# Batch norm with ReLU on one core: one tile of 32 rows per partition, and all loads then all stores on one queue

## Chip, cores, metric

One core of one Trainium2 chip. The metric is the device time of one execution in microseconds (us), lower is better. The granted clock was 1.00, so it plays no part. "Share" and "GB/s" of DMA mean the 16 DMA engines of the core together. In the views, ACT is the scalar engine, PE the tensor engine (PEld its weight loads), DVE the vector engine, POOL GpSimd and SP the sync engine. A load moves data from HBM (the chip's main memory) to SBUF (the core's own memory, 128 partitions), a store moves it back. "The turn" is the place in one queue where the first stores stand directly behind the last loads.

## The reference

```python
def setup_inputs():
    batch, channels, h, w = 32, 128, 32, 32        # x: 16.8 MB of float32
    ...
def reference(x, gamma, beta, running_mean, running_var, eps):
    normalized = (x - running_mean[None, :, None, None]) / np.sqrt(running_var[None, :, None, None] + eps)
    scaled = normalized * gamma[None, :, None, None] + beta[None, :, None, None]
    return np.maximum(scaled, 0).astype(np.float32)
```

x is 4,096 rows (batch x channel) of 1,024 numbers. Each row needs one scale and one bias, so a row is one ACT instruction: relu(scale * x + bias), 128 rows at a time, one in each partition. 16.8 MB go in and 16.8 MB come out.

## The kernel before

Two tiles of 16 rows per partition, loaded in pieces on the sync queue. ACT works in place and issues the stores from its own queue, so loads and stores run side by side. Cuts are marked.

```python
J = 16
PIECES = (((0, 2), (2, 4), (4, 8), (8, 16)), ((0, 8), (8, 16)))
STORE_CUTS = {(0, 1)}
...
    xr = x.rearrange("b c h w -> (b c) (h w)").rearrange("(t p j) w -> t p j w", p=P, j=J)
...
    for t in range(T):
        for a, b in PIECES[t]:
            xt = data.tile([P, b - a, HW], F32, name=f"x{t}_{a}")
            nc.sync.dma_start(out=xt, in_=xr[t, :, a:b, :])
            tiles.append((t, a, b, xt))
...     # parameters: four small loads on the scalar queue, one matmul that spreads them, sqrt, reciprocal, ...
    with tc.manual_schedule(engines={mybir.EngineType.Activation}):
        for t, a, b, xt in tiles:
            first = a
            for j in range(a, b):
                nc.scalar.activation(out=xt[:, j - a, :], in_=xt[:, j - a, :], func=ACTF.Relu,
                                     bias=bias_t[:, j : j + 1], scale=scale_t[:, j : j + 1])
                if j + 1 == b or (t, j + 1) in STORE_CUTS:
                    nc.scalar.dma_start(out=outr[t, :, first : j + 1, :], in_=xt[:, first - a : j + 1 - a, :])
                    first = j + 1
```

Of the kernel before, what the change touches and what calls it, by code (L numbers as in the profile page):

```python
# [1 line left out]

# [4 lines left out]


F32 = mybir.dt.float32
ACTF = mybir.ActivationFunctionType  # L10



J = 16

PIECES = (((0, 2), (2, 4), (4, 8), (8, 16)), ((0, 8), (8, 16)))

STORE_CUTS = {(0, 1)}


@with_exitstack
def kernel(
    ctx: ExitStack,
    tc: tile.TileContext,
    x: bass.AP,
    gamma: bass.AP,
    beta: bass.AP,
    running_mean: bass.AP,
    running_var: bass.AP,
    eps: bass.AP,  # L30
    out: bass.AP,
):
    nc = tc.nc
    B, C, H, W = x.shape
    HW = H * W
    P = nc.NUM_PARTITIONS
    assert C % J == 0 and P % (C // J) == 0 and (B * C) % (P * J) == 0
    Q = C // J
    T = B * C // (P * J)

    xr = x.rearrange("b c h w -> (b c) (h w)").rearrange("(t p j) w -> t p j w", p=P, j=J)
    outr = out.rearrange("b c h w -> (b c) (h w)").rearrange("(t p j) w -> t p j w", p=P, j=J)

    data = ctx.enter_context(tc.tile_pool(name="data", bufs=1))
    params = ctx.enter_context(tc.tile_pool(name="params", bufs=1))
    psum = ctx.enter_context(tc.tile_pool(name="psum", bufs=1, space=bass.MemoryType.PSUM))

    tiles = []
    for t in range(T):
        for a, b in PIECES[t]:  # L50
            xt = data.tile([P, b - a, HW], F32, name=f"x{t}_{a}")
            nc.sync.dma_start(out=xt, in_=xr[t, :, a:b, :])  # L52
            tiles.append((t, a, b, xt))



    raw = params.tile([Q, 4, J], F32, name="raw")
    for k, src in enumerate((running_var, gamma, running_mean, beta)):
        nc.scalar.dma_start(out=raw[:, k, :], in_=src.rearrange("(q j) -> q j", j=J))
    eps_t = params.tile([P, 1], F32, name="eps_t")  # L60
    nc.vector.memset(eps_t, float(eps))  # L61
    rep = params.tile([Q, P // Q, Q], F32, name="rep")
    nc.gpsimd.memset(rep, 1.0)  # L63
    nc.gpsimd.affine_select(  # L64
        out=rep,
        in_=rep,
        compare_op=mybir.AluOpType.is_equal,
        fill=0.0,
        base=0,
        pattern=[[0, P // Q], [-1, Q]],  # L70
        channel_multiplier=1,
    )
    cols = psum.tile([P, 4, J], F32, name="cols")
    nc.tensor.matmul(  # L74
        cols.rearrange("p k j -> p (k j)"),
        rep.rearrange("q r s -> q (r s)"),
        raw.rearrange("q k j -> q (k j)"),
        start=True,
        stop=True,
    )  # L80
    std_t = params.tile([P, J], F32, name="std_t")
    nc.scalar.activation(out=std_t, in_=cols[:, 0, :], func=ACTF.Sqrt, bias=eps_t[:, 0:1], scale=1.0)  # L82
    rstd_t = params.tile([P, J], F32, name="rstd_t")
    nc.vector.reciprocal(out=rstd_t, in_=std_t)  # L84
    scale_t = params.tile([P, J], F32, name="scale_t")
    nc.vector.tensor_mul(out=scale_t, in0=cols[:, 1, :], in1=rstd_t)  # L86
    ms_t = params.tile([P, J], F32, name="ms_t")
    nc.vector.tensor_mul(out=ms_t, in0=cols[:, 2, :], in1=scale_t)  # L88
    bias_t = params.tile([P, J], F32, name="bias_t")
    nc.vector.tensor_sub(out=bias_t, in0=cols[:, 3, :], in1=ms_t)  # L90

    with tc.manual_schedule(engines={mybir.EngineType.Activation}):
        for t, a, b, xt in tiles:
            first = a
            for j in range(a, b):
                nc.scalar.activation(  # L96
                    out=xt[:, j - a, :],
                    in_=xt[:, j - a, :],
                    func=ACTF.Relu,
                    bias=bias_t[:, j : j + 1],  # L100
                    scale=scale_t[:, j : j + 1],
                )
                if j + 1 == b or (t, j + 1) in STORE_CUTS:
                    nc.scalar.dma_start(
                        out=outr[t, :, first : j + 1, :], in_=xt[:, first - a : j + 1 - a, :]
                    )
                    first = j + 1


# [1 line left out]
_INS = ['x', 'gamma', 'beta', 'running_mean', 'running_var', 'eps']  # L111
_OUTS = [((32, 128, 32, 32), 'float32')]

_NUMBERS = {'eps': 1e-05}


# [26 lines left out]
```

## Time and profile before

| | before |
|---|---|
| time, median (range) | 83.86 us (83.78 to 83.91, 3 runs) |
| span of the profiled run | 81.9 us |
| DMA share, both queues | 96.2% |
| ACT busy | 38.5 us (47%) |

Read it as a DMA kernel: 33.56 MB through engines that are busy nearly all the time. The lines are in the prediction.

The view counts each packet whole in the stretch in which it begins. Of this kernel's stretches of 5 us some therefore read 367 and some 500 GB/s, but their DMA share goes along (0.86 and 1.16).

### The profile page before, as it was taken

What the parts mean: (1) busy time and instruction counts of PE and PEld (TensorE: products, weight loads), DVE (VectorE), ACT (ScalarE), POOL (GpSimd) and SP (SyncE); (2) the same over time, 40 slices, a digit from 0 to 9 for tenths busy, and PEclk for the clock granted to TensorE, in tenths of its full rate; (3) what the DMA queues carried; (4) which work ended last, traced back from release to release, by engine and by line L of the source; (5) the groups of instructions that cost most, each with busy time, mean ns of one, the idle gap of its engine ahead of it and who ended that gap; (6) DMA issues with size and microseconds to landing.
All of it is one profiled execution on the core that took longest, in us unless ns stands there. A gap on an engine that the chain in (4) does not pass through costs nothing.

```text
span 81.9 us, 119 instructions
## 1 busy us (share of the span) xinstructions
PE 0.7 (1%) x2; PEld 0.5 (1%) x2; DVE 0.8 (1%) x5; ACT 38.5 (47%) x34; POOL 0.8 (1%) x6
## 2 busy tenths in 40 slices
PE   0002000000000000000000000000000000000000
PEld 0002000000000000000000000000000000000000
DVE  0000300000000000000000000000000000000000
ACT  0600377799039999199994199993000000000000
POOL 3000000000000000000000000000000000000000
DMA  2899999989899999979789798996999899799690
GB/s 32 328 425 472 408 448 448 512 352 494 370 448 416 446 418 396 500 296 600 320 380 580 304 464 384 512 512 288 480 512 400 368 512 448 320 512 496 272 512 0
DMA packets 1936, 33.56 MB, mean 410 GB/s; under 512 B 272, under 2 KB 272, under 8 KB 528
## 3 DMA queue, kind: packets, MB, share of 16 engines
q1 hardware_dynamic: 864, 16.78, 48.4%
q10 hardware_dynamic: 1072, 16.78, 47.8%
HBM read 16.78 MB, written 16.78 MB: 410 GB/s over the span
## 4 chain that ended last, share of the span: by engine, by line
DMA 56%; ACT 11%; SPq 0%; issue 0%
DMA x<-in_x_dram 56%; ACT x L96 11%; SPq L52 0%
## 5 line engine op out<-in xcount | busy, mean ns | idle before, releaser
L96 ACT ACTIVATE x<-x,bias_t,scale_t 128x1024 f32<-128x1024 f32 x32 | 37.0, 1228 | 10.3 <-DMA x<-in_x_dram 7.9
L82 ACT ACT_TABLE_LOAD x1 | 1.3, 1283 | 2.6 <-issue 2.6
L82 ACT ACTIVATE std_t<-cols,eps_t 128x16 f32<-128x16 f32 x1 | 0.3, 273 | 4.5 <-PE cols L74 4.5
L74 PE MATMUL cols<-raw,rep 8*128 8x64 f32 x2 | 0.7, 428 | 7.7 <-DMA raw<-in_beta_dram 7.7
L74 PEld LDWEIGHTS cols<-raw,rep 8*128 8x128 f32 x2 | 0.5, 304 | 7.7 <-issue 7.7
L64 POOL TENSOR_SCALAR_AFFINE_SELECT rep<-rep 8x128 f32<-8x128 f32 x1 | 0.4, 392 | 0.1
L84 DVE RECIPROCAL rstd_t<-std_t 128x16 f32<-128x16 f32 x1 | 0.3, 254 | 7.8 <-ACT std_t L82 7.8
L63 POOL MEMSET rep<- 8x128 f32 x1 | 0.2, 195 | 0.3 <-POOLq L124 0.3
L86 DVE TENSOR_TENSOR scale_t<-cols,rstd_t 128x16 f32<-128x16 f32 x1 | 0.2, 175 | 0.1
L90 DVE TENSOR_TENSOR bias_t<-cols,ms_t 128x16 f32<-128x16 f32 x1 | 0.2, 175 | 0.0
L88 DVE TENSOR_TENSOR ms_t<-cols,scale_t 128x16 f32<-128x16 f32 x1 | 0.2, 175 | 0.0
L124 POOL MEMSET const-bfloat16-1.0<- 128x1 bf16 x1 | 0.1, 106 | 0.0
L124 POOL MEMSET const-uint8-127<- 128x1 uint8 x1 | 0.1, 106 | 0.0
L124 POOL MEMSET const-float32-0.0<- 128x1 f32 x1 | 0.1, 103 | 0.3 <-issue 0.3
L124 POOL MEMSET const-float32-1.0<- 128x1 f32 x1 | 0.1, 103 | 0.0
L61 DVE MEMSET eps_t<- 128x1 f32 x1 | 0.1, 59 | 0.9 <-PEq L124 0.9
## 6 DMA issues: line engine op xcount, KB each, us to landing
x<-in_x_dram SPq DMA_DIRECT2D x3, 4096.0 KB, 38.8
out_dram<-x ACTq DMA_DIRECT2D x3, 4096.0 KB, 27.9
x<-in_x_dram SPq DMA_DIRECT2D x2, 1024.0 KB, 5.7
x<-in_x_dram SPq DMA_DIRECT2D x1, 2048.0 KB, 11.2
out_dram<-x ACTq DMA_DIRECT2D x1, 2048.0 KB
out_dram<-x ACTq DMA_DIRECT2D x2, 512.0 KB, 18.8
out_dram<-x ACTq DMA_DIRECT2D x1, 1024.0 KB
raw<-in_running_var_dram ACTq DMA_DIRECT2D x1, 0.5 KB
```

The lines of the kernel that those rows point to most:

```text
L61: nc.vector.memset(eps_t, float(eps))
L63: nc.gpsimd.memset(rep, 1.0)
L64: nc.gpsimd.affine_select(out=rep, in_=rep, compare_op=mybir.AluOpType.is_equal, fill=0.0, base=0, pattern=[[0, P // Q], [-1, Q]], channel ...
L74: nc.tensor.matmul(cols.rearrange("p k j -> p (k j)"), rep.rearrange("q r s -> q (r s)"), raw.rearrange("q k j -> q (k j)"), start=True, s ...
L82: nc.scalar.activation(out=std_t, in_=cols[:, 0, :], func=ACTF.Sqrt, bias=eps_t[:, 0:1], scale=1.0)
L84: nc.vector.reciprocal(out=rstd_t, in_=std_t)
L86: nc.vector.tensor_mul(out=scale_t, in0=cols[:, 1, :], in1=rstd_t)
L88: nc.vector.tensor_mul(out=ms_t, in0=cols[:, 2, :], in1=scale_t)
L90: nc.vector.tensor_sub(out=bias_t, in0=cols[:, 3, :], in1=ms_t)
L96: nc.scalar.activation(out=xt[:, j - a, :], in_=xt[:, j - a, :], func=ACTF.Relu, bias=bias_t[:, j : j + 1], scale=scale_t[:, j : j + 1],)
L124: nc = _bacc.Bacc("TRN2", target_bir_lowering=False, num_devices=1)
```

## The change

The intent: fewer and larger packets, no mixing of reads and writes, and no DMA issues on ACT. All 32 rows of a partition are in one tile. The sync queue gets all loads, then all stores, and where the two meet the pieces are small so that neither has to wait long for the other.

```diff
-J = 16
+J = 32
-PIECES = (((0, 2), (2, 4), (4, 8), (8, 16)), ((0, 8), (8, 16)))
-STORE_CUTS = {(0, 1)}
+LOADS = ((0, 2), (2, 16), (16, 28), (28, 30), (30, 31), (31, 32))
+STORES = ((0, 1), (1, 2), (2, 4), (4, 16), (16, 28), (28, 32))
...
+    xt = data.tile([P, J, HW], F32, name="xt")
+    with tc.manual_schedule(engines={mybir.EngineType.SP}):
+        for a, b in LOADS:
+            nc.sync.dma_start(out=xt[:, a:b, :], in_=xr[0, :, a:b, :])
...
+    for j in range(J):
+        nc.scalar.activation(out=xt[:, j, :], in_=xt[:, j, :], ...)
+
+    with tc.manual_schedule(engines={mybir.EngineType.SP}):
+        for a, b in STORES:
+            nc.sync.dma_start(out=outr[0, :, a:b, :], in_=xt[:, a:b, :])
```

More of the change, by code (lines that the diff above doesn't have):

```diff
@@ L36 @@
     P = nc.NUM_PARTITIONS
-    assert C % J == 0 and P % (C // J) == 0 and (B * C) % (P * J) == 0
+    assert C % J == 0 and P % (C // J) == 0 and B * C == P * J
     Q = C // J
-    T = B * C // (P * J)
     xr = x.rearrange("b c h w -> (b c) (h w)").rearrange("(t p j) w -> t p j w", p=P, j=J)
@@ L46 @@
     psum = ctx.enter_context(tc.tile_pool(name="psum", bufs=1, space=bass.MemoryType.PSUM))
-    tiles = []
-    for t in range(T):
-        for a, b in PIECES[t]:
-            xt = data.tile([P, b - a, HW], F32, name=f"x{t}_{a}")
-            nc.sync.dma_start(out=xt, in_=xr[t, :, a:b, :])
-            tiles.append((t, a, b, xt))
     raw = params.tile([Q, 4, J], F32, name="raw")
@@ L90 @@
     nc.vector.tensor_sub(out=bias_t, in0=cols[:, 3, :], in1=ms_t)
-    with tc.manual_schedule(engines={mybir.EngineType.Activation}):
-        for t, a, b, xt in tiles:
-            first = a
-            for j in range(a, b):
-                nc.scalar.activation(
-                    out=xt[:, j - a, :],
-                    in_=xt[:, j - a, :],
-                    func=ACTF.Relu,
-                    bias=bias_t[:, j : j + 1],
-                    scale=scale_t[:, j : j + 1],
-                )
-                if j + 1 == b or (t, j + 1) in STORE_CUTS:
-                    nc.scalar.dma_start(
-                        out=outr[t, :, first : j + 1, :], in_=xt[:, first - a : j + 1 - a, :]
-                    )
-                    first = j + 1
+    for j in range(J):
+        nc.scalar.activation(
+            out=xt[:, j, :],
+            in_=xt[:, j, :],
+            func=ACTF.Relu,
+            bias=bias_t[:, j : j + 1],
+            scale=scale_t[:, j : j + 1],
+        )
+    with tc.manual_schedule(engines={mybir.EngineType.SP}):
+        for a, b in STORES:
+            nc.sync.dma_start(out=outr[0, :, a:b, :], in_=xt[:, a:b, :])
 _INS = ['x', 'gamma', 'beta', 'running_mean', 'running_var', 'eps']
```

## The prediction

> **What bounds the kernel now.** I looked first at the engines' busy time and the forty slices, then at the queues, the chain that ended last, the waits and the timeline.
>
> ```profile
> PE 0.7 (1%) x2; PEld 0.5 (1%) x2; DVE 0.8 (1%) x5; ACT 38.5 (47%) x34; POOL 0.8 (1%) x6
> ...
> DMA  2899999989899999979789798996999899799690
> ...
> q1 hardware_dynamic: 864, 16.78, 48.4%
> q10 hardware_dynamic: 1072, 16.78, 47.8%
> HBM read 16.78 MB, written 16.78 MB: 410 GB/s over the span
> ```
>
> ACT, the busiest compute engine, works 47% of the span. The two DMA queues (q1 is the sync queue with the loads, q10 the scalar queue with parameters and stores) together hold the sixteen DMA engines for 48.4 + 47.8 = 96.2% of the span. The DMA row is full from the second slice to the last but one. What is not DMA is a start, an end and little in between.
>
> ```profile
> L96 ACT ACTIVATE x<-x,bias_t,scale_t 128x1024 f32<-128x1024 f32 x32 | 37.0, 1228 | 10.3 <-DMA x<-in_x_dram 7.9
> ```
> ```profile
> 0.74 0.07 issue
> 0.81 0.37 SPq L52
> 1.18 0.05 issue
> 1.23 6.74 DMA x<-in_x_dram
> 7.97 0.02 issue
> 7.99 38.77 DMA x<-in_x_dram
> 46.76 0.03 issue
> 46.79 9.16 ACT x L96 x8
> ```
>
> The second view is the chain that ended last, by start and length. It stops at 56 us, where the last store is issued; the remaining 25 us are that store and those before it draining. ACT's 10.3 us of idle time are off the path: at 46.79 us ACT gets the last load, needs 9.16 us for its eight rows, and the stores already queued cover that.
>
> ```profile
> 30.00:46.70 16.70, 0.00 (x0) 0.00 (x0) 0.00 (x0) 12.17 (x11) 0.00 (x0) 1.00 1.01 430
> 46.70:60.00 13.30, 0.00 (x0) 0.00 (x0) 0.00 (x0) 9.16 (x8) 0.00 (x0) 1.00 1.05 452
> 60.00:80.00 20.00, 0.00 (x0) 0.00 (x0) 0.00 (x0) 0.00 (x0) 0.00 (x0) 1.00 0.98 421
> ```
>
> The last two columns of these stretches are DMA share and GB/s. Mixed reads and writes (first row) and writes alone (last row) move much the same; the differences are in how whole packets fall at the borders. So neither direction is cheaper alone, and mixing is nearly free.
>
> **The DMA sum, from the packet records of the trace.** A packet (one contiguous run of one partition) takes, median, 159 ns for 4,096 B, 309 for 8,192, 611 for 16,384 and 1,213 for 32,768, loads and stores alike: a line of 0.03678 ns per byte plus 8 ns. Each engine moves 33,554,432/16 = 2,097,152 B, so 77.13 us, and in this kernel 48 load and 56 store packets, 104 x 0.008 = 0.83 us: 77.96 us. First data packet to last packet's end measured 1.85 to 80.62 us, 78.77. The excess is 0.81 us: 0.44 is the slow start (8,192 B load packets average 337 ns, 28 over the median, x 16), 0.19 is mixing (32,768 B load packets average 1,221 ns instead of 1,213, x 24), 0.18 is gaps. Around that stand 1.85 us before the first packet, 0.35 to the last landing, 0.93 to the span's end, and 83.77 - 81.9 = 1.9 outside the span.
>
> **What the Trainium skill says.** "DMA: Bandwidth & Descriptors", section "Issuing engines are not separate DMA queues": DMAs started by different engines run on the same 16 DMA engines and interleave, so another issuer saves only issue time. The trace agrees: q1 and q10 add up to 96%, and issues take 0.34 us on ACT. The same page, "Where 436 GB/s comes from", puts the ceiling at 435 GB/s; 1/0.03678 x 16 = 435 agrees. Its section "Queues, rings and completion order" says an engine takes turns between queue rows packet by packet. That agrees too: the small parameter transfers landed about 0.63 us apart, two 309 ns packets. Its "Latency and other measured facts" tells of a loss from row pitches that are large powers of two (207 instead of 214 GB/s per direction at 512 KiB); this trace has only a 64 KiB pitch, at full rate, and the change makes it 128 KiB.
>
> **The change part by part.**
>
> Removed: seven store issues of about 0.34 us from ACT, and the 1.3 us that ACT waited for its own results before them. Off the path: worth 0 now.
>
> Packets: loads of 2, 14, 12, 2, 1 and 1 rows and stores of 1, 1, 2, 12, 12 and 4 rows, at 8 packets per engine each: 96 packets instead of 104 if nothing is cut up. 8 x 0.008 = 0.06 us less. A 14-row packet (57,344 B) should take 8 + 2,109 = 2.12 us, a 12-row packet 1.82.
>
> Mixing: gone, as the stores stand behind all loads in one queue. Takes away up to 0.19 us.
>
> The hand-over: new. Loads end at 1.85 + 0.44 + 38.57 + 48 x 0.008 = 41.2 us. Behind them each engine should go straight on with stores, if these are queued in time. The instruction order of the built program shows that dependencies are kept by piece: every store waits for a higher count of ACT's work (rows 1, 2, 4, 16, 28, 32), not for the whole tile. When are they ready?
> - Rows 0, 1: ACT starts after the parameters. 9.72 us before; now parameter packets take turns with 2.1 us packets instead of 0.3 us ones, so I estimate 12 to 19 us. Both done by about 22, far before 41.2.
> - Rows 2 to 15 land at 2.3 + 8 x 0.309 + 8 x 2.12 + about 0.8 = 22.5. At 1.145 us a row (9.16/8), rows 2 and 3 are done at 24.8, row 15 at 38.5.
> - Rows 16 to 27 have landed at 37.1, so ACT continues at once: done at 52.3. Rows 28 to 31: 56.9.
>
> The engines need the store of rows 2 to 3 at 41.2 + 16 x 0.159 = 43.8; of 4 to 15 at 43.8 + 2.5 = 46.2; of 16 to 27 at 46.2 + 14.5 = 60.8; of 28 to 31 at 75.3. An issue needs about 1 us to its first packet (0.81 to 1.85 before). Slack after that: 18, 6.7, 7.5 and 17 us. So no hole, with the tightest place at rows 4 to 15. I allow 0.15 us for the turn from load to store inside an engine, which no view shows.
>
> Sum: -0.06 - 0.19 + 0.15 = -0.1 us on 83.86, so 83.75; I say 83.7.
>
> **Rivals.**
> - Pure streams gain all the excess. If mixing, gaps and half of the slow start vanished: 83.86 - 0.06 - 0.19 - 0.18 - 0.2 = 83.2. The absolute floor with the ends as they are is 1.85 + 77.9 + 0.35 + 0.93 + 1.9 = 82.9, above the 82.2 that 2% would take. That bounds the chance of "faster" tightly. For it speaks only the equal per-packet time, against it that the slow start belongs to the first load, which is unchanged.
> - The turn costs a bubble. If the sync queue could not queue stores behind loads, or each engine drained its last writes before the first store read, one issue-to-packet delay of about 1 us is exposed: 84.8. Against it: stores queued behind loads on different queues show no hole today, and they are issued by 22 us.
> - ACT becomes the gate. Parameters would have to come after about 26 us to eat the 6.7 us of slack; then each us costs one. If it waited for all 32 rows, stores would start at 58 instead of 41 and the time would be about 100. The per-piece waits in the program speak against it.
> - The doubled pitch slows HBM. If the skill's 3% for 512 KiB applied already at 128 KiB: 78 x 0.03 = 2.3 us, 86.1. Nothing in the trace speaks for it, but nothing tests it.
>
> **Range and chances.** The bound is the same, the bytes are the same, the rate is at its ceiling before. So 83.7, with 83.1 to 84.6 holding the saving of all excess at one end and most of a bubble at the other. Faster by over 2% would break the floor: 0.02. Slower by over 2% (above 85.5) needs the pitch effect or a real starvation: 0.08. Within 2%: 0.90.
>
> **What would show it.** In the changed kernel's profile: one queue with nearly all bytes and a share near 96 to 97%; a DMA row with no low digit in the middle; ACT's first row later than 9.72 us, its last ending near 57 us; issues on the sync queue waiting for ACT without a hole in the DMA row after 41 us. Packets of 57,344 B at 2.12 us would prove the line, longer ones the pitch effect. A gap at 41 to 47 us would prove the bubble or the late ACT, and I would be wrong about the hand-over; a first data packet earlier than 1.85 us or a shorter end would be a gain I have not counted.

## More of the kernel before

One view is busy time by stretch. Its columns are stretch, length, five engines' busy time, clock, DMA share and GB/s.

```profile
4.00:38.00 34.00, 0.65 (x2) 0.49 (x2) 0.78 (x4) 22.10 (x20) 0.00 (x0) 1.00 1.01 430
38.00:44.00 6.00, 0.00 (x0) 0.00 (x0) 0.00 (x0) 5.97 (x6) 0.00 (x0) 1.00 1.01 437
44.00:80.00 36.00, 0.00 (x0) 0.00 (x0) 0.00 (x0) 9.16 (x8) 0.00 (x0) 1.00 1.01 433
```

About the same rate everywhere.

## The result, and the profile after

| | before | after |
|---|---|---|
| time, median (range), 6 runs each | 83.84 us (83.71 to 84.05) | 84.56 us (84.45 to 84.76) |
| ratio | 1 | 1.0087 (95% interval 1.0068 to 1.0106) |
| span of the profiled run | 81.9 us | 82.8 us |
| first data packet to end of last | 78.76 us | 79.83 us |

A ratio is the mean time of one kernel's fast runs over that of the other's of the same rounds, so not quite the ratio of the medians. The interval excludes 1: the change costs 0.7 us.

The page of the changed kernel, the parts that answer to those of before:

```profile
PE 0.8 (1%) x2; PEld 0.5 (1%) x2; DVE 1.0 (1%) x5; ACT 38.0 (46%) x34; POOL 0.9 (1%) x6
...
DMA  3799999999888899949999998889999888996990
...
q1 hardware_dynamic: 1728, 33.56, 96.0%
q10 hardware_dynamic: 32, 0.00, 0.0%
HBM read 16.78 MB, written 16.78 MB: 405 GB/s over the span
```

As intended, one queue carries all. Its packets still fill 96.0% of a span that became 0.9 us longer: the engines are not idle for the lost time, their packets take longer. That is the trap in this profile. A DMA share near the top says that packets are in flight, not that they go at full speed.

The chain that ended last, and the waits of the sync queue (line waited for: us in total, times, longest):

```profile
1.24 21.46 DMA xt<-in_x_dram
22.70 0.03 issue
22.73 21.60 ACT xt L90 x19
```
```profile
SPq L100 <- ACT xt L90: 44.9, 6, 13.2
```

The chain now runs through ACT, which works from 22.73 us without a break to 56.77. One could conclude that ACT has become the bound. It has not: the 44.9 us in which the sync queue waits for ACT before it issues stores pass while earlier transfers are in the queue. The landings show it. Rows 28 and 29, the last two-row load, land by 39.74 us; row 30 by 41.08 us; row 31 by 43.13; then the stores of row 0 by 44.46, row 1 by 45.70, rows 2 and 3 by 48.14. From then on each piece follows at full rate and there is no hole.

The same three stretches as before:

```profile
4.00:38.00 34.00, 0.76 (x2) 0.50 (x2) 0.93 (x4) 17.93 (x17) 0.00 (x0) 1.00 1.00 433
38.00:44.00 6.00, 0.00 (x0) 0.00 (x0) 0.00 (x0) 6.00 (x6) 0.00 (x0) 1.00 1.00 355
44.00:80.00 36.00, 0.00 (x0) 0.00 (x0) 0.00 (x0) 12.77 (x12) 0.00 (x0) 1.00 1.01 436
```

The first and last stretch run at 433 and 436 GB/s. The stretch in which the loads end and the stores begin has a DMA share of 1.00 and 355 GB/s. At 433 it would have moved 6 x 78 = 468 kB more, worth about 1.1 us. So the place is found.

The packet records say which packets. In this kernel the two last load pieces have 4,096 B packets (rows 30 and 31), and so have the two first stores. Mean time of a packet, in ns:

```
load of row 30    184.9
load of row 31    235.0
store of row 0    159.0
store of row 1    159.0      (159 is also the median of before)
```

It is the loads just ahead of the turn that are slow, up to 741 ns for a single one. The first stores go at nominal speed at once. The loss is 8 x (184.9 - 159) + 8 x (235.0 - 159) = 0.82 us per engine.

I use one sum for all runs below. "Extra" is the time of all data packets beyond 8 ns + 0.03678 ns per byte, per engine, by where it lies:

| us per engine | start (to 4 us) | beside other transfers | the turn | all |
|---|---|---|---|---|
| before | 0.42 | 0.20 | none | 0.62 |
| after | 0.65 | 0.01 | 0.82 | 1.47 |

The packets' own count changed by -0.06 us, the extra by +0.85, and what is left (78.76 - 77.97 - 0.62 = 0.17 before, 79.83 - 77.91 - 1.47 = 0.45 after) by +0.28: together the +1.07 of the table. The remainder may be the slowest engine against the mean one: the last store's sixteen landings lie 0.29 us apart before and 0.79 us after. About 0.3 us are given back outside the span and in the last wait: 84.53 - 82.8 = 1.7 us outside now, 1.9 before.

### The profile page after: what moved, and what is told of

It reads as the page before. It is cut to its first block, busy times and chain, and to the rows that moved or that the text cites. A ratio compares the mean times of both kernels' runs of the same rounds, so it can differ in the third digit from the quotient of the medians.

```text
span 82.8 us, 121 instructions
## 1 busy us (share of the span) xinstructions
PE 0.8 (1%) x2; PEld 0.5 (1%) x2; DVE 1.0 (1%) x5; ACT 38.0 (46%) x34; POOL 0.9 (1%) x6
## 4 chain that ended last, share of the span: by engine, by line
ACT 40%; DMA 26%; ACTq 1%; SPq 0%; issue 0%
ACT xt L90 40%; DMA xt<-in_x_dram 26%; ACTq L131 1%; SPq L55 0%
## 5 line engine op out<-in xcount | busy, mean ns | idle before, releaser
L90 ACT ACTIVATE xt<-xt,bias_t,scale_t 128x1024 f32<-128x1024 f32 x32 | 36.4, 1226 | 5.2 <-DMA xt<-in_x_dram 4.0
L71 PE MATMUL cols<-raw,rep 4*128 4x128 f32 x2 | 0.8, 482 | 14.1 <-DMA raw<-in_beta_dram 14.1
L71 PEld LDWEIGHTS cols<-raw,rep 4*128 4x128 f32 x2 | 0.5, 308 | 14.1 <-issue 14.1
L61 POOL TENSOR_SCALAR_AFFINE_SELECT rep<-rep 4x128 f32<-4x128 f32 x1 | 0.5, 508 | 0.1
```

The costliest lines, as they stand in the source:

```text
L61: nc.gpsimd.affine_select(out=rep, in_=rep, compare_op=mybir.AluOpType.is_equal, fill=0.0, base=0, pattern=[[0, P // Q], [-1, Q]], channel ...
L71: nc.tensor.matmul(cols.rearrange("p k j -> p (k j)"), rep.rearrange("q r s -> q (r s)"), raw.rearrange("q k j -> q (k j)"), start=True, s ...
L90: nc.scalar.activation(out=xt[:, j, :], in_=xt[:, j, :], func=ACTF.Relu, bias=bias_t[:, j : j + 1], scale=scale_t[:, j : j + 1],)
```

## The experiments

The prediction had named a bubble at the turn as a rival, so the first question was what kind of turn cost this is. Theories: **T**, every turn from reads to writes costs when all engines do it together; **S**, small packets at the turn are at fault; **L**, the tile (row pitch of 128 KiB instead of 64) or the later start is. Each run below was timed against before in the same rounds (before: 83.83 to 83.88 us medians). The changed kernel was not in these rounds, so a run is compared with it by the ratios to before (its own: 1.0087, 1.0068 to 1.0106). The extra at the turn comes from one profile of each kernel. With the same 4,096 B pieces at the turn it was 0.82 (after) and 1.02 to 1.12 (e5 to e7), so a difference of 0.3 us between runs is not read here.

| run | time us | ratio to before (95%) | extra at the turn, us per engine |
|---|---|---|---|
| e1_big_turn | 84.80 | 1.0105 (1.0089 to 1.0122) | 1.32 |
| e2_two_queues | 84.56 | 1.0077 (1.0061 to 1.0093) | no turn; 0.91 beside stores |
| e3_j16_one_queue | 84.94 | 1.0120 (1.0103 to 1.0138) | 1.53 |
| e4_three_turns | 85.03 | 1.0132 (1.0111 to 1.0152) | 1.55 first, 0.01 second |
| e5_warm_all | 84.82 | 1.0115 (1.0101 to 1.0128) | 1.12 |
| e6_warm_one_row | 84.61 | 1.0100 (1.0083 to 1.0117) | 1.02 |
| e7_warm_scratch | 84.69 | 1.0099 (1.0085 to 1.0113) | 1.07 |
| e8_before_warm | 84.74 | 1.0103 (1.0084 to 1.0123) | no turn; 0.76 beside stores |
| e9_early_turn | 85.08 | 1.0154 (1.0133 to 1.0174) | 1.51 first, 0.06 second |
| e10_sbuf_turn (2 executions) | 89.72 | 1.0697 (1.0671 to 1.0723) | 1.42 first, none second |
| e11_j32_mixed_small | 83.82 | 0.9996 (0.9980 to 1.0013) | no turn; 0.23 beside stores |
| e12_mix_then_turn | 84.47 | 1.0076 (1.0063 to 1.0090) | 0.84 |

### e1: large pieces where the two meet

```diff
-LOADS = ((0, 2), (2, 16), (16, 28), (28, 30), (30, 31), (31, 32))
-STORES = ((0, 1), (1, 2), (2, 4), (4, 16), (16, 28), (28, 32))
+LOADS = ((0, 2), (2, 16), (16, 28), (28, 32))
+STORES = ((0, 4), (4, 16), (16, 28), (28, 32))
```

> One load queue and one store order as in the changed kernel, but large packets where the two meet: last load 4 rows (16,384 B packets), first store 4 rows. Theory T (turning all engines from reads to writes at once costs about 0.8 us whatever the packet size): about 84.4 us, and the DMA rate still drops for about 2 us near 41 us. Theory S (the 4,096 B packets at the turn cannot cover the latency of the turn): the drop is gone, about 83.7 us. Theory L (the 128 KiB pitch or the slower start costs it): 84.4, without a change to the drop.

84.80 us, some 0.2 us more than the changed kernel, but the intervals of the ratios overlap; no theory had put it so high. The extra at the turn grew from 0.82 to 1.32, while 32 packets fewer per engine save 32 x 8 ns = 0.26 us. S falls: larger pieces do not take the drop away. Whether the small pieces of the change pay is not clear from this, and as the last load and the first store both changed, neither is singled out. The eight packets per engine of the last load (16,384 B, nominal 611 ns) took on average 611, 611, 611, 611, 694, 1,089, 1,185 and 790 ns. So the last four, 64 KiB per engine, are slow, as the last sixteen of 4,096 B were.

### e2: the stores back on the scalar queue

```diff
+            if j + 1 in ends:          # ends of STORES, pieces as in the changed kernel
+                nc.scalar.dma_start(out=outr[0, :, first : j + 1, :], in_=xt[:, first : j + 1, :])
-    with tc.manual_schedule(engines={mybir.EngineType.SP}):
-        for a, b in STORES: ...
```

> The changed kernel's tile, loads and store pieces, but the stores issued from the scalar queue as before, so that reads and writes mix from about 18 us. T and S both: no drop near 41 us, about 83.7 us (0.8 under the changed kernel). L: about 84.5, as the layout is unchanged. First landing of rows 0 and 1 at about 5.7 us if the later start belongs to the layout.

84.56 us, where T and S both said 83.7, and L about this. A miss for T as I had put it. The trace has no single drop: load packets are slow in three places, each just before the first packets of one of the small stores (0.18 us of extra in 57,344 B packets from 17 to 22 us, 0.56 in 49,152 B packets from 34 to 39, 0.15 in 8,192 B packets from 40 to 42). So either the tile or the large load pieces cost time in the two-queue form as well; e11 decides.

### e3: the kernel before, with its stores on the sync queue behind all loads

```diff
-                    nc.scalar.dma_start(out=outr[t, :, first : j + 1, :], in_=...)
+                    stores.append((t, first, j + 1, xt, a))
...
+    with tc.manual_schedule(engines={mybir.EngineType.SP}):
+        for t, first, end, xt, a in stores:
+            nc.sync.dma_start(out=outr[t, :, first:end, :], in_=xt[:, first - a : end - a, :])
```

> The kernel before with one change: stores on the sync queue behind all loads (tiles of 16 rows, 64 KiB pitch, loads 2,2,4,8,8,8 rows, stores 1,1,2,4,8,8,8). T: the drop at the turn appears, about 84.6 us. S: last loads are 32,768 B and first stores 4,096 B, so half of the drop, about 84.2. L: no loss, 83.8 us.

84.94 us, where T said 84.6: one part of the change alone, the stores in the loads' queue behind all loads, costs more than the whole change. The stretch view of this run:

```profile
4.00:38.00 34.00, 0.66 (x2) 0.50 (x2) 0.78 (x4) 24.44 (x23) 0.00 (x0) 1.00 1.02 439
38.00:44.00 6.00, 0.00 (x0) 0.00 (x0) 0.00 (x0) 3.90 (x4) 0.00 (x0) 1.00 0.89 269
44.00:80.00 36.00, 0.00 (x0) 0.00 (x0) 0.00 (x0) 8.56 (x8) 0.00 (x0) 1.00 1.01 436
```

269 GB/s in the middle, but with a share of only 0.89, because large packets that began before 38 us are counted in the first stretch. The packet times decide: the last two load packets of each engine, 2 x 32,768 B, took 1,987 and 1,967 ns instead of 1,213, all earlier ones 1,213 to 1,214, and all first stores exactly 159. Again the last 64 KiB of loads of each engine. The 64 KiB pitch does not save it, so L does not explain the drop.

### e4: four phases, with two turns from loads to stores

```diff
+LOADS = (((0, 2), (2, 12), (12, 24)), ((24, 32),))
+STORES = (((0, 8),), ((8, 16), (16, 24), (24, 32)))
```
(The sync queue gets the first loads, the first stores, the second loads, the second stores.)

> The changed kernel's tile and single queue, large packets only, but in four phases: loads of 24 rows, stores of 8, loads of 8, stores of 24, so two turns from reads to writes and one back. T with 0.8 us at each read-to-write turn: about 85.2 us; if the turn back costs as much, 86.0; drops in the DMA rate near 31, 41 and 51 us. S and L: no drops, 83.7 (S) or 84.5 (L).

85.03 us. The first turn (near 32 us) cost 1.55 us per engine; the turn back to loads and the second turn to stores (near 53 us) cost nothing, although the second store had been issued at 38.43 us and waited in the queue as the first had.

```profile
4.00:27.00 23.00, 0.76 (x2) 0.50 (x2) 0.93 (x4) 11.88 (x12) 0.00 (x0) 1.00 1.03 447
27.00:33.00 6.00, 0.00 (x0) 0.00 (x0) 0.00 (x0) 2.20 (x2) 0.00 (x0) 1.00 0.98 311
33.00:80.00 47.00, 0.00 (x0) 0.00 (x0) 0.00 (x0) 22.84 (x20) 0.00 (x0) 1.00 0.99 429
```

T as stated falls too: it is not every turn, but the first. That suggested a cold first write, theory C.

### e5, e6, e7, e8: touch the output early

One line ahead of the parameter loads; e5 as shown, e6 with one row only (`outr[0, 0:1, 0, 0:128]`), e7 into an unused HBM buffer of the same layout, e8 the same touch in the kernel before, for both of its tiles.

```diff
+    nc.scalar.dma_start(out=outr[0, :, 0, 0:128], in_=xr[0, :, 0, 0:128])
```

> The changed kernel with one small transfer more, first on the scalar queue: 512 B of x are copied straight into each partition's first output row (64 KB in all), and overwritten by the real store later, so the result stays right. Theory C (what costs 1 to 1.3 us at the first read-to-write turn, and nothing at the second one of the four-phase run, is the first touch of the output, and is paid once): the drop near 41 us vanishes, time about 83.7 us, or the loss moves to the first 5 us and the time stays at 84.6 with no drop at 41. Theory T2 (the turn itself costs when all engines turn together, and the four-phase run escaped it the second time for another reason): drop as before, 84.6.

> As the run that touches every partition's output, but only one 512 B spot of one row, written in 16 pieces by all 16 DMA engines. C by place (each part of the output has to be touched): drop near 41 us stays, 84.6 us. C by engine (the first write of each DMA engine is slow wherever it goes): drop gone, like the run that touches all. T2: drop stays, 84.6.

> As the run that touches every partition's output, but the 128 pieces of 512 B go to another HBM buffer of the same size and layout. C by place: drop stays, 84.6 us. C by engine or by direction: drop gone. T2: drop stays.

> The kernel before with the same first touch of each output row group (256 pieces of 512 B). It lost only about 0.2 us to slow load packets, spread over its mixed stretch. C: those slow packets (1,273 ns and more near 20, 31 and 35 us) go, and the time is 83.7 to 83.9; if the touch costs more than it saves, 84.1. T2: 83.9, with the slow packets still there.

84.82, 84.61 and 84.69 us, with 1.12, 1.02 and 1.07 us extra at the turn: the drop stays in all three. One line of e5's stretches:

```profile
38.00:44.00 6.00, 0.00 (x0) 0.00 (x0) 0.00 (x0) 6.00 (x7) 0.00 (x0) 1.00 0.98 328
```

C falls in all its forms that a small early write can test. The touch itself costs: its 512 B packets took 28 ns, so e5's eight per engine are 0.22 us, which is about what e5 lies above the changed kernel (84.82 - 84.56 = 0.26); e7, with as many such packets, lies only 0.13 above it, so this is not more than a fit. e8 was meant to gain a little on before and lost 0.9 us: 16 x 28 ns = 0.45 us for its packets, and 0.39 us more extra (1.01 against 0.62), most of it in load packets between 43 and 46.5 us, just ahead of the end of the loads. Why the early copy does that to the end of the loads, I did not find out.

### e9 and e10: what does the first turn turn to?

e9 is like e4 with two long load phases (loads of 16 rows, stores of 4, loads of 16, stores of 28). e10 has a copy between two SBUF tiles in place of the first stores; no store is issued before the last load has been. The result stays right.

```diff
 # e9
+LOADS = (((0, 2), (2, 8), (8, 16)), ((16, 24), (24, 32)))
+STORES = (((0, 4),), ((4, 8), (8, 16), (16, 24), (24, 32)))
 # e10, instead of the first stores
+                nc.sync.dma_start(out=sink, in_=zeros)      # [128, 4, 1024] each, SBUF to SBUF
```

> One queue, large packets, four phases with two long load phases: loads of 16 rows, stores of 4, loads of 16, stores of 28. Theory B (a one-off: until the first turn an engine's reads are only just in time; at the first turn its fast reads of the next stores crowd out the last loads, afterwards its reads stay ahead by a full buffer): a drop of 1 to 1.3 us of load time just before 21 us, none before 46 us, time about 84.9. Theory R (every turn after a long load phase costs): both drops, about 86.

> As the early-turn run, but the first burst is no store: a 2 MB copy between two SBUF tiles (zeros, unused), then loads of 16 rows, then all stores. Moves 2 MB more, so about 4.9 us longer than the early-turn run on that account. B: the loads just before the copy (about 21 us) are slow although nothing is written to HBM, and the turn to the stores (about 46 us) is free. Theory H (the first heavy writes to HBM, after the loads, cost it): the turn to the copy is free and the drop stands before the stores at about 46 us.

First e9, then e10:

```profile
4.00:18.00 14.00, 0.76 (x2) 0.50 (x2) 0.93 (x4) 7.00 (x7) 0.00 (x0) 1.00 1.02 438
18.00:24.00 6.00, 0.00 (x0) 0.00 (x0) 0.00 (x0) 2.44 (x3) 0.00 (x0) 1.00 1.00 322
24.00:80.00 56.00, 0.00 (x0) 0.00 (x0) 0.00 (x0) 27.47 (x24) 0.00 (x0) 1.00 1.00 432
```
```profile
4.00:18.00 14.00, 0.76 (x2) 0.50 (x2) 2.13 (x6) 8.29 (x8) 0.00 (x0) 1.00 1.01 434
18.00:24.00 6.00, 0.00 (x0) 0.00 (x0) 0.00 (x0) 2.57 (x4) 0.00 (x0) 1.00 1.02 339
24.00:80.00 56.00, 0.00 (x0) 0.00 (x0) 0.00 (x0) 27.35 (x24) 0.00 (x0) 1.00 1.00 432
```

The two lines in the middle are nearly the same. The loads ahead of the copy are slowed (1.42 us per engine) just as those ahead of the stores (1.51), with no HBM write near. And in both, the later turn to the stores is free (none and 0.06 us), though a load phase of about 20 us precedes it. So it isn't writing to HBM, not the first touch, and not the length of the load phase. What the slowed places have in common is that there, for the first time in the sync queue, transfers which read SBUF come directly behind transfers which read HBM. Theories R and H fall. B's places and times hold: 85.08 against "about 84.9", and e10 is 4.64 us longer than e9 against "about 4.9"; the drop itself, 1.51 and 1.42 us, is larger than its "1 to 1.3".

### e11: the one tile, with the queues and pieces of before

```diff
-LOADS = ((0, 2), (2, 16), (16, 28), (28, 30), (30, 31), (31, 32))
-STORES = ((0, 1), (1, 2), (2, 4), (4, 16), (16, 28), (28, 32))
+LOADS = ((0, 2), (2, 4), (4, 8), (8, 16), (16, 24), (24, 32))
+STORES = ((0, 1), (1, 2), (2, 4), (4, 8), (8, 16), (16, 24), (24, 32))     # from the scalar queue
```

> The kernel before's queues and piece sizes (loads 2,2,4,8,8,8 and stores 1,1,2,4,8,8,8 rows, stores from the scalar queue), with the changed kernel's one tile of 32 rows per partition. The two-queue run with the big load pieces lost 0.7 us against before. If that came from its packets of 57,344 and 49,152 B beside small stores: 83.9 here. If it came from the tile (128 KiB pitch): 84.5.

83.82 us against 83.83, ratio 0.9996. The tile and its 128 KiB pitch cost nothing that these runs resolve (95% interval 0.9980 to 1.0013). L is out, and e2's loss belongs to its piece sizes: same tile, same two queues, 84.56 with pieces of 14 and 12 rows and 83.82 with pieces of at most 8. Which of those pieces is to blame, a load or a store, is not separated.

```profile
4.00:38.00 34.00, 0.76 (x2) 0.50 (x2) 0.93 (x4) 22.22 (x20) 0.00 (x0) 1.00 1.01 429
38.00:44.00 6.00, 0.00 (x0) 0.00 (x0) 0.00 (x0) 5.87 (x6) 0.00 (x0) 1.00 1.01 437
44.00:80.00 36.00, 0.00 (x0) 0.00 (x0) 0.00 (x0) 9.16 (x8) 0.00 (x0) 1.00 1.01 433
```

### e12: a little mixing first, then the turn

e11 with only the stores of rows 0 and 1 on the scalar queue, early, and all others on the sync queue behind the loads.

```diff
+    ends = {b: a for a, b in STORES[:2]}       # these two from the scalar queue
...
+        for a, b in STORES[2:]:
+            nc.sync.dma_start(out=outr[0, :, a:b, :], in_=xt[:, a:b, :])
```

> The tile of 32 rows with the loads of the kernel before (2,2,4,8,8,8 rows); only the first two one-row stores on the scalar queue, early, beside the loads; all other stores (2,4,8,8,8 rows) on the sync queue behind all loads. Theory B (a one-off that small early stores among the loads pay cheaply): slow load packets of 0.2 us in total while the two stores run, no drop at the turn near 42 to 46 us, time 83.6 to 83.9, so at most 0.2 under both kernels. Theory M (mixing has to go on up to the last load): the drop stands at the turn, 84.6 to 84.9.

84.47 us, and 0.84 us extra at the turn, so B's hope that early mixing pays for the turn fails (the early stores do come with about 0.2 us of slow load packets, as B said). M named the place; the time lies just under its 84.6 to 84.9. This was the attempt at a version that beats both, and it does not.

```profile
38.00:44.00 6.00, 0.00 (x0) 0.00 (x0) 0.00 (x0) 5.86 (x6) 0.00 (x0) 1.00 0.99 366
```

The last two load packets of each engine are again the slow ones. The loss is smaller than e3's 1.53; but the first store behind the loads also differs (2 rows here, 1 row there), so I do not say what made it smaller. Two one-row stores of the *other* queue among the loads do not do for the sync queue what stores of its own do (e4, e9). But those were of 8 and 4 rows, so whether the queue or the amount makes the difference is not separated.

### What is shown, and what is not

Shown, in these runs: the cost appears at the first place in the sync queue where transfers that read SBUF stand directly behind loads from HBM, and in the three runs with a second such place it did not come again (e4, e9, e10). It falls on the last 64 KiB of loads of each engine (in e4, with 49,152 B packets, on the last two). It is 0.8 to 1.1 us with 4,096 B load packets, 1.3 with 16,384 B, and 1.4 to 1.6 with 32,768 and 49,152 B, except for e12: 0.84 with 32,768 B, after two early stores. So packet size alone does not set it. Neither the tile (e3) nor a small early write (e5 to e7) accounts for it.

Not shown: why. The Trainium skill, "DMA: Bandwidth & Descriptors", section "Two DMAs through the same engine are not ordered", says that descriptors of one queue are pipelined and that an engine's read and write sides are separate queues. A reading that fits: at the turn an engine already reads the next transfers from SBUF while its last loads are still coming from HBM, the two share its way in, and afterwards its reads stay ahead. The traces agree in that loads are slowed and stores are not (159.0 ns from the first), but they do not show the reads and writes apart. It stays an inference. A rival to it was not tried: that the end of the first pure run of loads is slow whatever stands behind it; no run lets such loads end with nothing behind them. Open as well are e8's late loss and which piece slowed e2.

## Why the prediction was right or wrong

The class ("within 2%", given 0.90) was right, and the time, 84.56, lies in the range of 83.1 to 84.6, at its very edge. The direction was wrong: I said 0.1 us faster, it is 0.7 us slower. That the time still lies in the range is owed to the rival of the bubble, for which the range had been stretched upward, not to the sum. By steps:

- *Packets, -0.06 us: right.* 57,344 B took 2,116 ns (predicted 2.12 us), 49,152 B took 1,815 (1.82).
- *Mixing, up to -0.19: right.* The extra beside other transfers fell from 0.20 to 0.01 us.
- *No starvation: right.* ACT's first row began at 16.38 us (predicted 12 to 19), rows 2 to 15 had landed at 22.73 (22.5), ACT ended at 56.77 (56.9). No store was late.
- *The hand-over, +0.15: wrong, and this is the step that failed.* "I allow 0.15 us for the turn from load to store inside an engine" was an allowance without a measurement. It measured 0.82 us of slow load packets per engine, and the engines came out of this run further apart (0.79 us between the last landings, 0.29 before). The step had asked only whether the stores would be ready in time. They were; the loads ahead of them slowed.
- *Unmoved start: not settled.* The start cost 0.65 us extra in the profile after and 0.42 before, but single profiles of the experiments range from 0.26 to 0.49, so 0.23 us may be chance.
- *The rivals.* "The turn costs a bubble", 84.8, had the right place and nearly the right size. Its picture was wrong: I expected an idle gap and said a gap in the DMA row would show it. The engines stay busy and the packets get slow. The DMA row does have a low digit, the 4 near 36 us, but that is only the view's counting of packets where they begin: laid out by their own start and end, the packets fill that slice. The pitch rival is refuted by e11, ACT as the gate by the landings, the "pure streams" gain by the turn.

The argument against the bubble was the weak point: that "stores queued behind loads on different queues show no hole today" says nothing of one queue. The mixed kernel has no place where stores stand directly behind loads in one queue (on the scalar queue the parameters landed by 7.6 us and the first store was issued at 10.99), so its trace could not show what one costs.

## What to carry to other kernels

When a kernel is at its DMA ceiling, loads and stores on separate queues avoid the turn; here all stores behind all loads in one queue cost 1.2% (e3). Separate queues alone are not enough: with pieces of 12 and 14 rows they lost 0.7 us (e2), with pieces of at most 8 rows nothing (e11). Keeping the two apart agrees with the Trainium skill, "Perfetto Trace Analysis", section "DMA Optimizations", which suggests one issuer for inputs and another for outputs. If all must go through one queue, expect to pay at the first turn, 0.8 to 1.6 us here. Small pieces around it lose less there (0.82 to 1.12 us against 1.32), but their added packets cost 0.26 us, so the gain is small and not clear of the noise. When a DMA-bound span grows while the DMA share stays put, compare packet times or GB/s by stretch, not the share.

## What the Trainium skill lacked or had wrong

- "DMA: Bandwidth & Descriptors" has nothing on a cost where one queue first goes from HBM-sourced to SBUF-sourced transfers: 0.82 to 1.55 us of slowed load packets per engine (after, e1, e3 to e7, e9, e10, e12), and no second such cost in the runs with two turns (e4, e9, e10).
- The same page, "Issuing engines are not separate DMA queues", says that issuing from several engines saves only sequencer time. Here moving the stores to the loads' queue, behind all loads, and nothing else cost 1.1 us (84.94 against 83.88, e3), with no issue late.
- The same page, "Latency and other measured facts", warns of large power-of-two row pitches and gives no figure under 512 KiB. At 128 KiB against 64 KiB there was no difference: 83.82 against 83.83 us (e11).
- No page says how packets in two queues slow each other, by their size: load and store pieces of 12 and 14 rows instead of at most 8 cost 0.7 us (84.56 against 83.82, e2 and e11).
